# Four reorderings in a two-layer decoder kernel: copies ahead of a weight split, gate columns ahead of sums, sums behind a low part, and the last block in three pieces

## The chip, the cores and the metric

The kernel runs on one core of one Trainium2 chip. The metric is device microseconds (us) of one execution. A core has five engines with a queue each: TensorE (PE in the profile) multiplies matrices, VectorE (DVE), ScalarE (ACT) and GpSimd (POOL) work elementwise, and SyncE (SP) issues transfers. Each engine takes its instructions strictly in the order in which they were recorded, and waits on semaphores for the others.

## The reference

A trunk of two decoder layers over a residual stream `h` of 512 tokens by 1024 features, in float32. Each sublayer is normed before and after ("sandwich").

```python
for l in range(DEPTH):                       # DEPTH = 2
    g = norm_gains[l]
    if l < N_A:                              # layer 0: 12 heads in three groups (window, dilation)
        mix = dilated_mixer(rms_norm(h, g[0]), w_qkv_a[l], w_o_a[l], cos, sin)
    else:                                    # layer 1: 16 heads, keys and values from kvf
        if l == N_A:
            kvf = rms_norm(h, kv_norm) @ w_kvf
            ...
            log_f = jax.nn.log_sigmoid((kvf[..., 2 * B_WIDTH:] + b_f).astype(jnp.float32))
            c_sh = jnp.cumsum(log_f, axis=1) # gates: a bias c_q - c_k on the scores
        mix = fox_mixer(rms_norm(h, g[0]), w_q_b[j], w_o_b[j], k_sh, v_sh, c_sh)
    h = h + rms_norm(mix, g[1])
    f = conv_ffn(rms_norm(h, g[2]), w_up[l], conv_w[l], conv_b[l], w_down[l])
    h = h + rms_norm(f, g[3])
```

`conv_ffn` is an up projection to 5632 features, a causal convolution of width 3, a GELU gate, and a down projection from 2816 features.

## The kernel before

**Products in three passes.** A float32 product is made of three matmuls on operands that are split into a high part in fp32r and a low part, `mm3`: high by high, high by low, low by high (lines 276, 277, 278). So most of TensorE's rows come in threes. A weight piece of 128x1024 is loaded by SP (line 48) into a raw buffer; ACT casts it into the high part (line 56) and DVE subtracts that from the raw piece to get the low part (line 64). The class `Weights` does this ahead of need: `get()` hands out the next piece and first splits on until `ahead - 1` further pieces are ready; `split(n)` splits until `n` pieces are.

**Order by hand.** No scheduler moves anything: the order in which the Python code records instructions is the order on each engine. PSUM has eight banks of 128x512 float32; a new bank tile waits until the readers of the one before it in that bank are done.

**Place 1, layer 0's last projection.** `wide_proj(1, "v_ps", ...)` makes the values of two head groups in four banks and four steps `s`, each with one weight piece and 24 matmuls of 128x512. After each step stands a list of small work for the attention ("between"). In step 1 it is: transposes of queries and keys for blocks 2 and 3 of group 2 (`qk_transpose`, line 1045, each with a DVE copy out of PSUM, line 1048); scores of blocks 0 and 1 (`scores`, line 1072: two banks per block, then DVE's fused mask and minimum at line 1055 and ACT's exponential at line 1056); the transposes of block 3's probabilities of group 1 (`p_transpose`, line 1092, copied out by ACT at line 1094). The four banks that the values leave free serve all of these in turn. At the end of each step `next(down0)` does one stage of `down_sums`: sums and differences of quarters of the down-projection weights for a seven-product (Strassen-like) scheme, four DVE operations of 128x512 (lines 606 to 609), with loads by SP and stores to DRAM (`dT`, line 614).

**Place 2, the gates.** Before the second attention, the cumulative gates of 16 heads (tile `c8`) are transposed by TensorE (line 1620) and copied by DVE to `cq` (line 1622), a column for each head. POOL's `f_bias` (lines 1635, 1636) makes the bias of a score block from `cq` and `ck`. Here `down_sums` for layer 1 (`down1`) has its stores issued by POOL.

**Place 3, the end of the second attention.** The loop over 18 steps `m` ends with `f_out_low(7)` (line 1715), the low part of the last two heads' outputs, which is also the last reader of the bank `o_ps`. Then come the transposes of the convolution's columns (line 586) with their DVE copy (line 588), and the output projection `po.finish`, whose first `get()` splits eight pieces: four of `w_o_b`, four of `w_up`. The last of four sets of `down1` sums stood at `m = 17`, ahead of `f_out_low(7)`.

**Place 4, the last rows.** In the down projection of the last layer, the blocks of 128 tokens are finished in the order 2, 3, 0, 1. For a block, `p_11` makes the last nine matmuls of its first 512 columns and `p_12` those of the other 512. `Final` then squares and sums (ACT, line 316), multiplies by the gain (DVE, line 323: tile `mix`), and when the row's sum is known takes the root (ACT, 318), the reciprocal (DVE, 328), adds to `h` in two halves (DVE, 330) and stores each half (SP). For the last block, `narrow` cuts `p_12` into two parts of 256 columns, both in one bank.

Of the kernel before, what the change touches and what calls it, by code (L numbers as in the profile page):

```python
# [100 lines left out]
def trunk_kernel(ctx, tc, x, norm_gains, w_qkv_a, w_o_a, w_q_b, w_o_b, kv_norm, w_kvf, b_f,  # L101
# [199 lines left out]
    class Mix:  # L301
# [5 lines left out]
        def half(self, b, n, hf, o):  # L307
            if n == 0:
                self.st[b] = (small(2, "ss"), t4([128, D], name="mix"), small(1, "sd"), small(1, "vr"))
            self.part(b, n, o, H2[hf], n == 1)  # L310

        def part(self, b, n, o, s, last):

            ss, m, sd, v = self.st[b]
            junk = t2([128, 512], BF16, name="junk")
# [220 lines left out]
    class Final:  # L536
# [11 lines left out]
        def half(self, i, n, hf, o):  # L548
            self.mix.half(self.order[i], n, hf, o)
            if n:  # L550
                self.out(self.order[i])

        def part(self, b, n, o, s):
            self.mix.part(b, n, o, slice(512 + s.start, 512 + s.stop), n == 2)
            if n == 2:
                self.out(b)

# [73 lines left out]
    def ffn(l, bd, cp, nxt, ahead):  # L631
# [208 lines left out]
        def down(nxt, ahead):  # L840
# [39 lines left out]
            for i, b in enumerate(nxt.order):  # L880
                if ahead and i < 2:
                    W.split(W.n_split + 1)
                if b >= 2:
                    nxt.half(i, 0, 1, db[b, 1])
                    for j in range(ND - 2, ND):
                        p_21(j, b - 2)
                    nxt.half(i, 1, 0, db[b, 0])
                    for bp in range(2):
                        p_1(last[0] - 2 + i, bp)
                    if ahead and i == 1:  # L890
                        W.split(W.n_split + 1)
                    continue
                for j in last:
                    p_11(j, b)
                nxt.half(i, 0, 0, db[b, 0])
                parts = (slice(0, 256), slice(256, 512)) if nxt.narrow and i == NB - 1 else (slice(0, 512),)
                for q, part in enumerate(parts):
                    for j in last:
                        p_12(j, b, part)
                        if (i, j) == (NB - 1, last[1]) and getattr(nxt, "early", None):  # L900
                            nxt.early()
                    if len(parts) > 1:
                        nxt.part(b, 1 + q, db[b, 1][:, part], part)
                    else:
                        nxt.half(i, 1, 1, db[b, 1])

# [337 lines left out]

    def wide_proj(g, name, post, between):

        banks = [bank([128, T], name=name) for _ in range(4)]
        for s in range(4):
            w = W.get()
            wh, wl = (t.rearrange("p (k c) -> p k c", k=2) for t in w)  # L1250
            for b in range(4):
# [10 lines left out]
    def v_post(g, b, o):  # L1262
# [20 lines left out]
        [L(qk_transpose, 2, 0), L(qk_transpose, 2, 1), L(p_transpose, 1, 2)],  # L1283
        [L(qk_transpose, 2, 2), L(qk_transpose, 2, 3), L(scores, 2, 0), L(scores, 2, 1), L(p_transpose, 1, 3)],
        [L(scores, 2, 2), L(scores, 2, 3), L(p_transpose, 2, 0)],
        [factors, L(p_transpose, 2, 1), L(p_transpose, 2, 2), L(p_transpose, 2, 3)]])
    for g in range(2):
# [308 lines left out]
    for c in range(4, 8):  # L1596
# [17 lines left out]
        if c < 6:  # L1614
            next(gate)
        if c >= 6:
            next(down1)
# [3 lines left out]
    cq = sml.tile([128, 4, 16], F32, tag="cq", name="cq", bufs=1)  # L1621
    dve.tensor_copy(cq, cqp)
    load_ck(0)

# [105 lines left out]
    for m in range(M + 2):  # L1730
# [38 lines left out]
        if live and i0 == 2 and j:  # L1769
            f_out_low(j - 1)  # L1770
        if m >= M - 3:
            next(down1)

    f_out_low(7)
    W.ahead, W.ahead_dma = 4, 2
    cp = conv_columns(load_conv(1))
    bd = Boundary(load_gain(norm_gains[1, 1], "gain11"), load_gain(norm_gains[1, 2], "gain12"), "xc")
    po.finish(bd, 4)
# [45 lines left out]
```

## Time and profile before

| | |
|---|---|
| median of 3 runs | 1118.95 us (1118.54 to 1121.36) |
| the profiled execution | 1118.97 us, of which the span from first to last instruction is 1117.2 us |
| PE busy | 1104.7 us (99%), 6395 matmuls |
| DVE, ACT, POOL busy | 893.9 us (80%), 616.4 us (55%), 191.2 us (17%) |
| granted TensorE clock, mean | 0.996 |
| PE's waits in all | 6.2 us, in eight places |

Times in the profile's rows are us from the span's start. A timeline row gives start, duration, engine, line, operation, what it writes and reads, and in brackets the idle time before it and what ended that. Matmuls overlap: a row of 128x512 is shown with 0.39 us, and the next starts 0.23 us later. So work is counted here from start to start. A matmul on float32 operands (transposes, layer 0's scores) counts twice in the trace's numbers.

### The profile page before, as it was taken

How to read it: one execution, taken by the hardware profiler on the slowest of the kernel's cores; microseconds unless marked ns; L12 is line 12 of the kernel's file. 1: busy time of each engine (PE TensorE's matmuls, PEld its weight loads, DVE VectorE, ACT ScalarE, POOL GpSimd, SP SyncE). 2: the span in 40 equal slices, each digit the busy share in tenths (PEclk: the TensorE clock that was granted, in tenths of full speed). 3: DMA queues.
4: the chain of work that ended last, by engine and by line, in shares of the span. 5: the costliest groups of instructions: out<-in, count | busy, mean ns of one | idle time of the engine just before them, and what ended most of it. 6: DMA issues, size and time to landing. Idle time of an engine off the chain costs nothing.

```text
span 1117.2 us, 17530 instructions
## 1 busy us (share of the span) xinstructions
PE 1104.7 (99%) x6395; PEld 942.9 (84%) x6395; DVE 893.9 (80%) x1462; ACT 616.4 (55%) x1038; POOL 191.2 (17%) x287
## 2 busy tenths in 40 slices
PE   9999999999999999999999999999999999999997
PEld 6988789989989988888888788788889889888886
DVE  6577778888788589897877866968888888689994
ACT  5444466444454456576655677746545445456572
POOL 1832010400000121000010555411200000121000
PEclk9999999999999999999999999999999999999999
DMA  9469864334344499975762644894333443599862
GB/s 324 148 216 407 325 173 116 113 95 124 114 140 124 130 352 372 336 282 133 208 151 76 192 131 124 272 307 132 95 110 108 137 124 117 158 347 376 310 245 75
DMA packets 180464, 218.40 MB, mean 195 GB/s; under 512 B 11225, under 2 KB 131017, under 8 KB 180378
## 3 DMA queue, kind: packets, MB, share of 16 engines
q1 hardware_dynamic: 168698, 180.81, 49.1%
q0 software_dynamic: 11680, 36.48, 11.3%
q8 instruction: 50, 0.82, 0.3%
q14 instruction: 36, 0.29, 0.1%
HBM read 170.28 MB, written 39.63 MB: 188 GB/s over the span
## 4 chain that ended last, share of the span: by engine, by line
PE 92%; DVE 3%; ACT 2%; issue 1%; DMA 1%; SPq 0%; POOL 0%; DVEq 0%; ACTq 0%; POOLq 0%
PE up L276 13%; PE up L277 13%; PE up L278 13%; PE acc L276 7%; PE acc L278 7%; PE acc L277 7%; PE v_ps L276 2%; PE v_ps L277 2%; PE v_ps L278 2%; PE qk_ps L277 2%; PE qk_ps L276 2%; PE qk_ps L278 2%; PE first L278 1%; PE first L277 1%; PE first L276 1%; PE o_ps L1701 1%
## 5 line engine op out<-in xcount | busy, mean ns | idle before, releaser
L640 ACT ACTIVATE bb<-up,conv 128x512 f32<-128x512 f32 x80 | 60.6, 775 | 149.1 <-DVE up L967 76.2
L64 DVE TENSOR_TENSOR w<-wraw,w 128x1024 fp32r<-128x1024 f32 x94 | 121.1, 1314 | 26.5 <-ACT w L56 25.2
L56 ACT CAST w<-wraw 128x1024 fp32r<-128x1024 f32 x108 | 110.3, 1049 | 20.8 <-DMA wraw<-in_w_up_dram 8.1
L276 PE MATMUL acc<-w 128*128 128x512 f32 (+1 forms) x311 | 120.7, 388 | 1.1 <-DVE mix L323 1.1
L278 PE MATMUL acc<-w 128*128 128x512 f32 (+1 forms) x311 | 120.5, 387 | 0.0
L276 PE MATMUL up<-xch,w 128*128 128x512 f32 (+1 forms) x292 | 104.9, 359 | 0.0
L276 PE MATMUL up<-xbh,w 128*128 128x512 f32 (+1 forms) x292 | 104.9, 359 | 0.0
L277 PE MATMUL up<-xbl,w 128*128 128x512 f32 (+1 forms) x292 | 104.9, 359 | 0.0
L277 PE MATMUL up<-xcl,w 128*128 128x512 f32 (+1 forms) x292 | 104.9, 359 | 0.0
L278 PE MATMUL up<-xch,w 128*128 128x512 f32 (+1 forms) x292 | 104.7, 359 | 0.0
L278 PE MATMUL up<-xbh,w 128*128 128x512 f32 (+1 forms) x292 | 104.7, 359 | 0.0
L277 PE MATMUL acc<-w 128*128 128x512 f32 (+1 forms) x267 | 103.3, 387 | 0.0
L656 POOL DMA_DIRECT2D hD<-hc x42 | 24.2, 576 | 317.7 <-DVE hc L658 316.6
L276 PEld LDWEIGHTS acc<-w 128*128 128x128 f32 x311 | 58.4, 188 | 13.0 <-DVE mix L323 1.3
L278 PEld LDWEIGHTS acc<-w 128*128 128x128 f32 x311 | 58.4, 188 | 12.4 <-DVE w L768 0.4
L641 DVE SCALAR_TENSOR_TENSOR bb<-up,conv,bb 128x511 f32<-128x511 f32 x80 | 59.4, 743 | 7.8 <-ACT bb L640 7.8
L276 PE MATMUL up<-xsh,w 128*128 128x256 f32 x224 | 63.4, 283 | 0.0
L277 PE MATMUL up<-xsl,w 128*128 128x256 f32 x224 | 63.4, 283 | 0.0
L278 PE MATMUL up<-xsh,w 128*128 128x256 f32 x224 | 63.4, 283 | 0.0
L276 PEld LDWEIGHTS up<-xbh,w 128*128 128x128 f32 x292 | 55.1, 189 | 8.3
L643 DVE SCALAR_TENSOR_TENSOR bb<-up,conv,bb 128x510 f32<-128x510 f32 x80 | 59.9, 749 | 2.8
L276 PEld LDWEIGHTS up<-xch,w 128*128 128x128 f32 x292 | 55.1, 189 | 8.2
(325 smaller groups left out, 3032.8 us busy)
## 6 DMA issues: line engine op xcount, KB each, us to landing
wraw<-in_w_up_dram SPq DMA_DIRECT2D x88, 512.0 KB, 4.2
dT<-dsums SPq DMA_DIRECT2D x24, 512.0 KB, 6.5
dsums<-in_w_down_dram SPq DMA_DIRECT2D x22, 512.0 KB, 6.0
dsums<-in_w_down_dram SPq DMA_DIRECT2D x44, 256.0 KB, 7.2
hD<-hc POOLq DMA_DIRECT2D x44, 256.0 KB, 4.6
dact<-hD SPq DMA_DIRECT2D x44, 256.0 KB, 5.9
wraw<-dT SPq DMA_DIRECT2D x22, 512.0 KB, 7.3
wraw<-in_w_down_dram SPq DMA_DIRECT2D x22, 512.0 KB, 5.8
```

What stands on the lines that cost most here:

```text
L56: self.nc.scalar.copy(pair[:, 0], raw)
L64: self.nc.vector.tensor_tensor(pair[:, 1], raw, pair[:, 0].bitcast(F32), ALU.subtract)
L276: pe.matmul(o, ah, bh, start=first, stop=False, skip_group_check=shared)
L277: pe.matmul(o, ah, bl, start=False, stop=False, skip_group_check=shared)
L278: pe.matmul(o, al, bh, start=False, stop=last, skip_group_check=shared)
L640: act.activation(bb[:, s, :], ps, AF.Identity, bias=cp[:, 3, ch:ch + 1], scale=cp[:, 2, ch:ch + 1])
L641: dve.scalar_tensor_tensor(bb[:, s, 1:], ps[:, :T - 1], cp[:, 1, ch:ch + 1], bb[:, s, 1:], ALU.mult, ALU.add)
L643: dve.scalar_tensor_tensor(bb[:, s, 2:], ps[:, :T - 2], cp[:, 0, ch:ch + 1], bb[:, s, 2:], ALU.mult, ALU.add)
L656: pool.dma_start(hD[c - 1], hc.pop(c - 1))
L1701: pe.matmul(o[64 * hh:64 * hh + 64, i * 128:(i + 1) * 128], Vt[hd // 8][:, k, (hd % 8) * 64:(hd % 8) * 64 + 64], pT[j, i, hh][:, k, :], st ...
```

## The change

Four edits, each of order; no arithmetic is added or left out but one tiny add.

1. In step 1 of the value projection, `get()` splits one piece less (`ahead` 3 instead of 4). The piece is split later in the same step by `W.split(W.n_get + 3)`, which now stands behind the copies of the transposed queries and keys and behind `p_transpose(1, 3)`; that one is moved ahead of the scores.
2. The last `down1` stage before the second attention stands behind the transposes and the copy to `cq`, not ahead of them.
3. The last of the four `down1` stages in the attention's loop stands behind `f_out_low(7)` and the copy of the convolution's columns.
4. The last block's columns are made and treated as 512 to 768, then 0 to 512, then 768 to 1024, so that another bank's products lie between the two parts of one bank. The add and the stores of the block before are recorded behind the first of these pieces.

```diff
@@ class Mix
         def half(self, b, n, hf, o):
+            self.part(b, n, o, H2[hf], n == 1)
+
+        def part(self, b, n, o, s, last):
+
             if n == 0:
                 self.st[b] = (small(2, "ss"), t4([128, D], name="mix"), small(1, "sd"), small(1, "vr"))
-            self.part(b, n, o, H2[hf], n == 1)
-
-        def part(self, b, n, o, s, last):
...
@@ class Final
             self.mix.half(self.order[i], n, hf, o)
-            if n:
+            if n and i != 2:
                 self.out(self.order[i])
 
         def part(self, b, n, o, s):
-            self.mix.part(b, n, o, slice(512 + s.start, 512 + s.stop), n == 2)
-            if n == 2:
-                self.out(b)
+            self.mix.part(b, n, o, s, n == 2)
+            if n != 1:
+                self.out(b if n else self.order[2])
@@ def down
+                if nxt.narrow and i == NB - 1:
+                    for n, (start, stop) in enumerate(((512, 768), (0, 512), (768, 1024))):
+                        for j in last:
+                            if start:
+                                p_12(j, b, slice(start - 512, stop - 512))
+                            else:
+                                p_11(j, b)
+                        o = db[b, 1][:, start - 512:stop - 512] if start else db[b, 0]
+                        nxt.part(b, n, o, slice(start, stop))
+                    continue
...
@@ wide_proj
+            W.ahead = 3 if s == late else 4
             w = W.get()
+            W.ahead = 4
...
-        [L(qk_transpose, 2, 2), L(qk_transpose, 2, 3), L(scores, 2, 0), L(scores, 2, 1), L(p_transpose, 1, 3)],
+        [L(qk_transpose, 2, 2), L(qk_transpose, 2, 3), L(p_transpose, 1, 3), lambda: W.split(W.n_get + 3),
+         L(scores, 2, 0), L(scores, 2, 1)],
...
-        [factors, L(p_transpose, 2, 1), L(p_transpose, 2, 2), L(p_transpose, 2, 3)]])
+        [factors, L(p_transpose, 2, 1), L(p_transpose, 2, 2), L(p_transpose, 2, 3)]], 1)
@@ before the second attention
-        if c >= 6:
+        if c == 6:
             next(down1)
     cqp = bank([128, 4, 16], name="cq_ps")
...
     dve.tensor_copy(cq, cqp)
+    next(down1)
     load_ck(0)
@@ the attention's loop
-        if m >= M - 3:
+        if M - 3 <= m <= M:
             next(down1)
 
     f_out_low(7)
     W.ahead, W.ahead_dma = 4, 2
     cp = conv_columns(load_conv(1))
+    next(down1)
```

At place 1, DVE's queue around the copies of the transposed queries and keys (`qkT`), before. `dsums` are the weight sums, `w<-wraw,w` is the low part of a weight piece, and the row with the mask is the first operation on the scores:

```order
L607 TENSOR_TENSOR dsums<-dsums 128x512
L608 TENSOR_TENSOR dsums<-dsums 128x512
L609 TENSOR_TENSOR dsums<-dsums 128x512
L64 TENSOR_TENSOR w<-wraw,w 128x1024
L1048 COPY qkT_1200<-qkT_ps 128x512 x2
L1055 ISA p,st<-s_ps,mask_132 128x128
```

And with the change:

```order
L607 TENSOR_TENSOR dsums<-dsums 128x512
L608 TENSOR_TENSOR dsums<-dsums 128x512
L609 TENSOR_TENSOR dsums<-dsums 128x512
L1053 COPY qkT_1200<-qkT_ps 128x512 x2
L64 TENSOR_TENSOR w<-wraw,w 128x1024
L1060 ISA p,st<-s_ps,mask_132 128x128
```

The low part now stands between the copies and the scores' first operation. On ACT, the copy of `p_transpose(1, 3)` moves ahead of this piece's cast and of the exponentials of the scores; on PE, its transposes move ahead of the scores.

At place 2, DVE's queue at the end of the key projection, before (`cq` is the gates' columns, `kst` the last keys):

```order
L1376 TENSOR_TENSOR kst_5792<-k_ps,kst_5792 128x512
L606 TENSOR_TENSOR dsums<-dsums 128x512
L607 TENSOR_TENSOR dsums<-dsums 128x512
L608 TENSOR_TENSOR dsums<-dsums 128x512
L609 TENSOR_TENSOR dsums<-dsums 128x512
L1622 COPY cq<-cq_ps 128x64
L64 TENSOR_TENSOR w<-wraw,w 128x1024
```

And with the change:

```order
L1384 TENSOR_TENSOR kst_5792<-k_ps,kst_5792 128x512
L1630 COPY cq<-cq_ps 128x64
L606 TENSOR_TENSOR dsums<-dsums 128x512
L607 TENSOR_TENSOR dsums<-dsums 128x512
L608 TENSOR_TENSOR dsums<-dsums 128x512
L609 TENSOR_TENSOR dsums<-dsums 128x512
L64 TENSOR_TENSOR w<-wraw,w 128x1024
```

The copy is now ahead of the four sums. POOL's queue is the same in both: the two stores of these sums, then the first `f_bias`.

At place 4, the end of DVE's queue, before (`mix` is the row by its gain, `vr` the running sum of squares, `h` the output rows):

```order
L320 TENSOR_SCALAR vr<-ss 128x1
L323 TENSOR_TENSOR mix<-acc,gain_7819 128x512 x2
L328 RECIPROCAL rs<-sd 128x1
L330 TENSOR_SCALAR h<-mix,rs,h 128x512 x2
L320 TENSOR_SCALAR vr<-ss 128x1
L323 TENSOR_TENSOR mix<-acc,gain_7819 128x512
L322 TENSOR_TENSOR vr<-vr,ss 128x1
L323 TENSOR_TENSOR mix<-acc,gain_7819 128x256 x2
L328 RECIPROCAL rs<-sd 128x1
L330 TENSOR_SCALAR h<-mix,rs,h 128x512 x2
```

And with the change:

```order
L320 TENSOR_SCALAR vr<-ss 128x1
L323 TENSOR_TENSOR mix<-acc,gain_7819 128x512 x2
L320 TENSOR_SCALAR vr<-ss 128x1
L323 TENSOR_TENSOR mix<-acc,gain_7819 128x256
L328 RECIPROCAL rs<-sd 128x1
L330 TENSOR_SCALAR h<-mix,rs,h 128x512 x2
L322 TENSOR_TENSOR vr<-vr,ss 128x1
L323 TENSOR_TENSOR mix<-acc,gain_7819 128x512
L323 TENSOR_TENSOR mix<-acc,gain_7819 128x256
L328 RECIPROCAL rs<-sd 128x1
L330 TENSOR_SCALAR h<-mix,rs,h 128x512 x2
```

The block before the last has its reciprocal and its two adds between the first and the second piece of the last block. On PE, the nine matmuls of 128x256 of the first piece now stand ahead of the nine of 128x512, and the other nine of 128x256 behind them.

More of the change, by code (lines that the diff above doesn't have):

```diff
@@ L895, in down @@
                 nxt.half(i, 0, 0, db[b, 0])
[L896 to L905, printed above, removed]
+                for j in last:
+                    p_12(j, b)
+                    if (i, j) == (NB - 1, last[1]) and getattr(nxt, "early", None):
+                        nxt.early()
+                nxt.half(i, 1, 1, db[b, 1])
         def half_mm(o, w, x, s, start):
@@ L1243, in trunk_kernel, with wide_proj @@
     reorder(2, 3)
-    def wide_proj(g, name, post, between):
+    def wide_proj(g, name, post, between, late=None):
         banks = [bank([128, T], name=name) for _ in range(4)]
         for s in range(4):
+            W.ahead = 3 if s == late else 4
             w = W.get()
+            W.ahead = 4
             wh, wl = (t.rearrange("p (k c) -> p k c", k=2) for t in w)
```

## The prediction

> **What bounds the kernel now.** I read the page first, then PE's waits.
>
> ```profile
> PE 1104.7 (99%) x6395; PEld 942.9 (84%) x6395; DVE 893.9 (80%) x1462; ACT 616.4 (55%) x1038; POOL 191.2 (17%) x287
> PE s_ps L1072 <- DVE qkT L1048: 1.2, 1, 1.2
> PE acc L276 <- DVE mix L323: 1.1, 1, 1.1
> PE qk_ps L277 <- DVE w L64: 1.0, 2, 0.8
> PE o_ps L1701 <- ACT pT L1688: 0.7, 1, 0.7
> PE xt_ps L344 <- DVE xn L295: 0.4, 1, 0.4
> PE acc L276 <- DVE OTb L1715: 0.4, 1, 0.4
> ```
>
> The first row is TensorE's share of the span of 1117.2 us: 99%. The others give whom PE waited for: us in total, times, the longest. So no change of order can win more than PE's idle time, 6.2 us with the wait at the start, and what those waits cost beyond their own length. Four of these rows are the places of the four edits: `qkT` (place 1), `pT` (place 2), `OTb` (place 3), `mix` (place 4). Next I read place 1 on PE's timeline, and the granted clock in the windows around it.
>
> ```profile
> 119.19 0.72 PE L1072 MATMUL s_ps<-qkT 64*128 64x128 f32 x8
> 121.15 1.68 PE L1072 MATMUL s_ps<-qkT 64*128 64x128 f32 x8 [1.24 <-DVE qkT L1048]
> 130.01 1.26 PE L1072 MATMUL s_ps<-qkT 64*128 64x128 f32 x16
> 131.32 0.66 PE L1092 MATMUL pT_ps<-ident,p 128*128 128x128 f32 x4
> 137.29 1.47 PE L1092 MATMUL pT_ps<-ident,p 128*128 128x128 f32 x12
> ...
> 122.00:123.00 1.00, 1.00 (x5) 0.78 (x5) 1.00 (x11) 1.00 (x5) 0.00 (x0) 0.50 0.91 240
> 120.00:130.00 10.00, 8.85 (x36) 7.12 (x36) 7.29 (x24) 4.61 (x18) 0.00 (x0) 0.83 1.02 381
> 630.00:640.00 10.00, 9.22 (x63) 7.20 (x62) 9.81 (x32) 8.55 (x24) 8.58 (x16) 1.00 0.57 147
> ```
>
> In the window rows the number behind the five engines is the granted clock. PE stands still for 1.24 us ahead of the scores of block 1, since the third bank they need still holds transposes that DVE has not copied. Right behind that the clock is 0.50. Over 120 to 130 it is 0.83, which makes (1 - 0.83) x 10 / 0.5 = 3.4 us at half speed, a loss of 1.7 us. The wait of 0.74 us at 635 left the clock at 1.00.
>
> What the place costs in all: from 130.01 to 137.29 PE does the same work as from 119.19 to 130.01 (16 score passes, 4 transposes, 24 products), in 7.28 us. From 119.19 it took 10.82. So the stall with its slow clock costs 3.54 us, not 1.24.
>
> **Place 1: the copies first.** What PE waits for is DVE, which waits for ACT:
>
> ```profile
> 119.27 1.23 DVE L64 TENSOR_TENSOR w<-wraw,w 128x1024 fp32r<-128x1024 f32 x1 [2.72 <-ACT w L56]
> 120.41 1.28 DVE L1048 COPY qkT<-qkT_ps 128x512 f32<-128x512 f32 x2
> 121.61 0.28 DVE L1055 CUSTOM_DVE_ANT_0 p<-s_ps,mask 128x128 f32<-128x128 f32 x1
> 123.30 0.69 DVE L606 TENSOR_TENSOR dsums<-dsums 128x512 f32<-128x512 f32 x1
> 126.63 1.23 DVE L64 TENSOR_TENSOR w<-wraw,w 128x1024 fp32r<-128x1024 f32 x1 [0.46 <-ACT w L56]
> 130.75 0.29 DVE L1055 CUSTOM_DVE_ANT_0 p<-s_ps,mask 128x128 f32<-128x128 f32 x1 [2.90 <-PE s_ps L1072]
> ...
> 121.99 0.40 ACT L1056 ACTIVATE p<-p,st 128x128 f32<-128x128 f32 x1 [2.75 <-DVE st L1055]
> 125.09 0.56 ACT L1094 COPY PT<-pT_ps 128x512 f32<-128x512 f32 x1
> 125.55 1.05 ACT L56 CAST w<-wraw 128x1024 fp32r<-128x1024 f32 x1
> ```
>
> DVE had been idle for 2.72 us when it began the low part at 119.27, and only then came the copies. With the change they start when the transposes are there, the last by 119.2 (PE's next row starts at 119.19), and at 0.6 each (120.41 to 121.61 for both) they end by about 120.1, while PE does four transposes (0.42 from 131.32 to its next products) and the first scores. Bank by bank: the second score bank needs the first copy (about 119.5), the third the second copy (120.1), the fourth ACT's copy of `p_transpose(1, 3)`, done about 120.3. PE asks for them at about 119.9, 120.2 and 120.5, so the old wait is gone, and PE reaches the scores of step 2 at 119.19 + 7.28 = 126.47 instead of 130.01.
>
> What is late next is DVE, because the low part now stands between the copies and the scores' mask. I follow it with the durations above. The four transposes start at 119.19, their row is 0.66 long: ACT copies from 119.85, 0.46 later (125.09 to 125.55) it casts, from 120.31. The low part starts 1.08 after its cast (125.55 to 126.63): 121.39. The mask starts 1.14 behind it (119.27 to 120.41): 122.53, that is 0.92 later than before. The sums follow 1.69 behind (121.61 to 123.30), at 124.22, and take 2.87 (123.30 to 126.63 less the 0.46 of idling): 127.09. On ACT the exponentials start 0.38 behind the mask (121.61 to 121.99), at 122.91, and take 3.10; the next cast is at 126.01 and the next low part at 127.09. So the mask of step 2's scores can start at 127.09 + 1.14 = 128.23, where PE would have its scores ready from 126.47 on.
>
> Step 2's transposes need the bank of the first of these scores, and ran 0.57 behind the mask (130.75 to 131.32): 128.80. Undisturbed PE would be there 1.31 after the scores' start (130.01 to 131.32), at 127.78. So a **new wait of 1.02 us** takes the place of the old one, and PE is there at 128.80 instead of 131.32: **a gain of 2.52 us**. DVE and ACT are ahead by the same, and what follows follows them. The ends: 3.54 without a new wait, 0.8 if the new wait brings the half-speed stretch along (1.7 more). I take 2.52: the wait at 635, 0.74, left the clock alone, and 1.02 is not far above it.
>
> [...]
>
> **Place 2: gate columns first.**
>
> ```profile
> 623.54 0.69 DVE L609 TENSOR_TENSOR dsums<-dsums 128x512 f32<-128x512 f32 x1
> 624.15 0.22 DVE L1622 COPY cq<-cq_ps 128x64 f32<-128x64 f32 x1
> 624.29 1.21 DVE L64 TENSOR_TENSOR w<-wraw,w 128x1024 fp32r<-128x1024 f32 x1
> ...
> 624.53 0.53 POOL L614 DMA_DIRECT2D dT<-dsums  x1 [0.92 <-DVE cq L1622]
> 625.10 0.99 POOL L1635 TENSOR_SCALAR bias<-ck,cq 128x128 f32<-128x128 f32 x2
> ```
>
> `cq` is moved ahead of the sums on DVE, but POOL, which needs it, has the two stores of these very sums ahead of its first `f_bias`. The second store starts 0.30 behind the last sum's end (624.23), and the bias at once behind the store. So the bias never waited for `cq`, it waited for the sums. These now start 0.14 later (624.15 to 624.29, the copy). POOL, then DVE, then ACT pass this on to `pT`, and the wait at 635 grows from 0.74 to 0.88: **a loss of 0.14 us**. The ends: 0 and 0.3 (the copy's full 0.22 and a semaphore). A gain is excluded as long as POOL's order stands.
>
> **Place 3: the low part first.**
>
> ```profile
> 731.08 0.58 ACT L1711 CAST OTb<-o_ps 128x512 fp32r<-128x512 f32 x1 [2.39 <-PE o_ps L1701]
> 732.67 0.68 DVE L1715 TENSOR_TENSOR OTb<-o_ps,OTb 128x512 fp32r<-128x512 f32 x1
> 730.00:740.00 10.00, 9.58 (x59) 7.60 (x56) 8.12 (x10) 4.59 (x5) 1.59 (x3) 1.00 1.04 391
> 739.82 9.28 DMA wraw<-in_w_up_dram
> 756.48 0.76 DVE xn L295
> ```
>
> The second row is `f_out_low(7)`, for whose bank PE waits 0.42. It needs ACT's cast in the first row, which ends at 731.66; with one set of four sums less ahead of it, it can start by then, 1.01 earlier, and the wait goes. But the rows from the chain that ended last run elsewhere: from the load of a `w_up` piece (landing at 749.10) over its cast and low part to the normed rows `xn` at 756.48, for which PE waits 0.4 again (`xt_ps`). DMA is full at that time (share 1.04 from 730 to 740), and the bytes are the same. So PE comes 0.42 earlier to a point that does not come earlier: the wait there becomes 0.84, **a gain of 0**. The ends: 0.42 gained if DMA lands that much earlier, 1.86 lost if the moved sums (2.87 of DVE, less the 1.01) hold up the eight low parts behind them, thereby the raw buffers, and thereby the loads. I take 0, since DMA with a share above 1 is the nearer bound on that load.
>
> **Place 4: three pieces.**
>
> ```profile
> 1107.59 0.28 PE L276 MATMUL acc<-w 128*128 128x256 f32 x1
> 1108.54 0.28 PE L278 MATMUL acc<-w 128*128 128x256 f32 x1
> 1109.91 0.39 PE L276 MATMUL acc<-w 128*128 128x256 f32 x1 [1.09 <-DVE mix L323]
> 1110.97 0.28 PE L278 MATMUL acc<-w 128*128 128x256 f32 x1
> ...
> 1107.26 1.42 DVE L330 SCALAR_TENSOR_TENSOR h<-mix,rs,h 128x512 f32<-128x512 f32 x2
> 1111.84 0.42 DVE L323 TENSOR_TENSOR mix<-acc,gain 128x256 f32<-128x256 f32 x1 [1.98 <-ACT junk L316]
> ```
>
> These are the first and the last matmul of each part of 256 columns, then the add of the block before, and `mix` of the last part. The first part takes 0.95 from its first to its last start, 0.12 per matmul, so the second could have started at 1108.66. It started at 1109.91, 1.25 later, and took 1.06 from first to last: 1.36 us lost in all, since both parts lie in one bank that `mix` still read. In the new order nine matmuls of 512 (9 x 0.23 = 2.0 us) lie between, and `mix` of a part ends 1.3 after the part's last matmul started (1110.97 to 1112.26). Cover 2.1 against need 1.3: the wait goes, and the rows behind the last matmul are the same. The postponed add of the block before fits into those 2 us on DVE (1.42 us, which now runs ahead of the second piece's `mix`). **A gain of 1.36 us**; the ends are 1.0, if DVE's queue holds the last `mix` by 0.3, and 1.5.
>
> **The sum.** The profiled execution took 1118.97 us, as good as the median of 1118.95. 1118.97 - 2.52 + 0.14 - 0 - 1.36 = 1115.23: **1115.2 us**, 0.33% less. A measurement of this kernel can tell about 0.3% from no change, that is 3.36 us, with the line at 1115.6. The forecast lies just beyond it.
>
> **The rivals.**
> - **A, as summed** (chance 0.49): 1115.2, own range 1114.6 to 1116.0 from the small ends at places 2 to 4.
> - **B, no new wait at place 1** (0.12): DVE or ACT are quicker than the rows chained above. 1115.2 - 1.0 = 1114.2. Against it: each link is a row of the same stage.
> - **C, the slow stretch stays** (0.20): the new wait drops the clock as the old one did, or the timed runs of before did not all have the drop. 1.7 us less is won: 1116.9. For it: 1.02 us is not far from 1.24 either. Against the second form: two of the three times of before, 1118.54 and 1118.95, lie at the profiled one or 0.4 below, less than a drop. [...]
> - **D, place 3 holds up the loads** (0.08): 1115.2 + 1.86 = 1117.1. It decides from the point at which the raw buffers, not DMA, set the loads. For it: eight low parts are queued behind the moved sums. Against it: the share of 1.04.
> - **E, slower than before: the clock gives way at three waits** (0.05). Three waits are left or made: 1.02 at place 1, 0.88 at 635, 0.84 at 757. If from 0.8 us of idling on the clock drops for 3.4 us, each costs 1.7: 1115.2 + 5.1 = 1120.3, 0.12% above the median. It decides from the length of idling that drops the clock. Against it: 0.74 at 635 and the 0.8 in the row of `qk_ps` are nearly there, and I saw the drop behind the 1.24 alone.
> - **The change does not do what it says**: so it is at place 2, and that is in the sum. At places 1, 3 and 4 the queues do carry the new order.
>
> The rest (0.06) is unnamed, 0.04 of it slower. Faster by over 0.3%: 0.35 of A, all of B, 0.02 unnamed: 0.49. Within 0.3%: 0.14 of A, C, D, E: 0.47. Slower: 0.04. The range takes in A to D with 0.3 on both sides: 1113.9 to 1117.3.
>
> **What would show it.** Place 1: no wait for `qkT`; the clock at 1.00 between 118 and 126; a wait of about 1 us of the transposes `pT_ps` (line 1097) for DVE near 127.8; the `qkT` copies ending by 120.2. If that wait is under 0.4, the chain on DVE is wrong; if the clock falls behind it, C holds. Place 2: the first bias starts 0.1 to 0.2 later against the keys' last product, and the wait for `pT` is 0.8 to 1.0. Place 3: no wait for `OTb`, one of about 0.8 for `xn`. Place 4: no wait for `mix`, and the span's end 1.3 sooner behind the start of the last block. A total under 1113.9 would mean that a wait I count as renewed has gone for good; one over 1117.3, that a wait I do not see was made.

## The result, and the profile after

The change runs in **1115.89 us** (median of 7 runs, 1114.56 to 1118.54), the kernel before, beside it, in 1120.55 us (7 runs, 1118.54 to 1121.36). The ratio is 0.9969, with a 95% interval of 0.9958 to 0.9981: 0.3% faster, 0.7 us above the forecast of 1115.2 and inside its range. Between these medians the gain is 4.7 us, and 3.3 in the second series of the change below; the forecast, reckoned from the profiled 1118.97, was 3.7. Two runs of several ms, one of the kernel before and one of an experiment, are left out of all counts. The first profiled execution was the slowest of the seven, 1118.54 us, and that turned out to be instructive. PE's row and its waits in it (total, times, longest):

```profile
PE 1103.4 (99%) x6395; PEld 942.6 (84%) x6395; DVE 894.4 (80%) x1462; ACT 617.0 (55%) x1038; POOL 191.1 (17%) x287
PE xt_ps L344 <- DVE xn L295: 2.1, 1, 2.1
PE acc L278 <- DVE w L768: 1.1, 1, 1.1
PE pT_ps L1097 <- DVE st L1060: 0.8, 1, 0.8
PE o_ps L1710 <- ACT pT L1697: 0.7, 1, 0.7
```

The waits for `qkT`, `OTb` and `mix` are gone. `pT_ps` (line 1097) is the new wait forecast at place 1. `xt_ps` is 2.1 instead of the forecast 0.84, and the wait for a low part at line 768 is in no step of the prediction. Place 1 on the timeline, DVE first and then PE; next the clock (the number behind the engines) at place 1 and behind the wait for `xn`:

```profile
118.81 1.29 DVE L1053 COPY qkT<-qkT_ps 128x512 f32<-128x512 f32 x2 [2.30 <-PE qkT_ps L1050]
121.25 1.23 DVE L64 TENSOR_TENSOR w<-wraw,w 128x1024 fp32r<-128x1024 f32 x1 [1.15 <-ACT w L56]
122.39 0.28 DVE L1060 CUSTOM_DVE_ANT_0 p<-s_ps,mask 128x128 f32<-128x128 f32 x1
126.95 1.23 DVE L64 TENSOR_TENSOR w<-wraw,w 128x1024 fp32r<-128x1024 f32 x1
128.09 0.28 DVE L1060 CUSTOM_DVE_ANT_0 p<-s_ps,mask 128x128 f32<-128x128 f32 x1
...
119.58 1.45 PE L1077 MATMUL s_ps<-qkT 64*128 64x128 f32 x16
126.63 1.26 PE L1077 MATMUL s_ps<-qkT 64*128 64x128 f32 x16
128.74 0.63 PE L1097 MATMUL pT_ps<-ident,p 128*128 128x128 f32 x4 [0.85 <-DVE st L1060]
...
120.00:130.00 10.00, 9.15 (x62) 7.45 (x59) 8.74 (x40) 6.87 (x27) 0.00 (x0) 1.00 1.02 396
750.00:760.00 10.00, 7.85 (x31) 6.02 (x30) 8.51 (x17) 7.50 (x17) 0.00 (x0) 0.83 0.06 22
```

At place 1 the copies end at 120.10, the low part, the mask and the second low part follow as forecast, and PE waits 0.85 without losing the clock. Near 756 the clock is at half speed (0.50 in each us from 757 to 759) for (1 - 0.83) x 10 / 0.5 = 3.4 us, behind the 2.1 us of idling. The tail of the span, in order of time: the last matmul of the first piece, the first and last of the middle one, the first of the last piece, then `mix` of the last pieces:

```profile
1107.41 0.28 PE L278 MATMUL acc<-w 128*128 128x256 f32 x1
1107.53 0.40 PE L276 MATMUL acc<-w 128*128 128x512 f32 x1
1109.37 0.39 PE L278 MATMUL acc<-w 128*128 128x512 f32 x1
1109.60 0.28 PE L276 MATMUL acc<-w 128*128 128x256 f32 x1
...
1110.59 1.25 DVE L323 TENSOR_TENSOR mix<-acc,gain 128x512 f32<-128x512 f32 x2
```

No piece waits for the one before it. Every trace holds the same 6395 matmuls, so matmul k of one can be set against matmul k of another. Only inside places 1 and 4 does the change alter their order: matmul 632 is one of the scores in the kernel before and one of the transposes moved ahead of them in the change, but the gains come out the same, within 0.01, if they are reckoned from matmul 628, ahead of both. (In these counts only the scores' matmuls at place 1 stand twice. A transpose stands once: four for one `p_transpose`.) This table is worked out from the starts of single matmuls: where each execution stands against the profiled one of before, in us (a negative number is earlier). Several of its rows are experiments, told below.

```
ahead of / behind      place 1     place 2   place 3 at OTb  at xn  xn +12  l.768: before, behind  last block: first, last  
matmul no.            632    689   3500 3540   4200   4360    4452    4520     5900     5940          6360     6394
start in before    119.41 131.32 629.22 635.85 714.27 735.84 757.28  769.44   999.18  1008.51       1103.73  1110.97
change, 1st profile  -0.04  -2.58  -2.50 -2.50  -2.50  -3.50   -1.78   -0.16   -0.19     0.91          0.91    -0.42
change, 2nd profile  -0.33  -2.88  -2.47 -2.48  -2.47  -3.47   -3.06   -3.05   -3.08    -1.98         -1.97    -3.30
place 1 alone         0.71  -1.83  -1.75 -1.75  -1.75  -2.03   -2.17   -2.17   -2.18    -1.21         -1.20    -1.20
place 3 alone         0.19  -1.37  -1.29 -1.26  -1.27  -1.99   -2.08   -2.09   -2.12    -1.20         -1.21    -1.21
place 4 alone         0.11   0.13   0.21  0.23   0.24   0.22    0.17    0.17    0.15     1.72          1.72     0.39
change less place 3   0.14  -2.41  -2.34 -2.32  -2.32  -2.61   -2.96   -2.96   -2.98    -1.39         -1.40    -2.73
all mended            0.11  -3.14  -3.03 -3.86  -2.99  -3.96   -4.54   -4.82   -4.84    -5.10         -5.12    -6.45
```

The first column differs by what happens in the first 15 us of each execution (up to 0.7; the reason was not followed). A difference between two columns is what a stretch gives or costs.

### The profile page after: what moved, and what is told of

It is laid out like the page before. It is cut to its first block, busy times and chain, and to the rows that moved or that the text cites. A ratio compares the mean times of both kernels' runs of the same rounds, so it can differ in the third digit from the quotient of the medians.

```text
span 1116.7 us, 17530 instructions
## 1 busy us (share of the span) xinstructions
PE 1103.4 (99%) x6395; PEld 942.6 (84%) x6395; DVE 894.4 (80%) x1462; ACT 617.0 (55%) x1038; POOL 191.1 (17%) x287
## 4 chain that ended last, share of the span: by engine, by line
PE 90%; DMA 4%; ACT 2%; DVE 2%; issue 1%; SPq 1%; POOL 0%; DVEq 0%; ACTq 0%; POOLq 0%
PE up L276 12%; PE up L277 12%; PE up L278 12%; PE acc L276 8%; PE acc L278 8%; PE acc L277 8%; DMA dsums<-in_w_down_dram 2%; PE qk_ps L277 2%; PE qk_ps L276 2%; PE qk_ps L278 2%; PE v_ps L276 2%; PE v_ps L277 2%; PE v_ps L278 2%; PE o_ps L1710 2%; PE pT_ps L1695 2%; PE s_ps L1663 1%
```

## The experiments

**The edits one by one.** Place 1 alone, place 4 alone, place 3 alone, and the change without place 3: each takes the lines of the change's diff for its places and leaves the others as in the kernel before. Every experiment was timed beside its own runs of the kernel before, whose medians range from 1119.0 to 1120.4. So between two experiments, differences of about 1 us are read from the traces and not from the times; the intervals of the ratios of the change and of its single mends all overlap. Place 1:

```diff
-        [..., L(scores, 2, 0), L(scores, 2, 1), L(p_transpose, 1, 3)],
+        [..., L(p_transpose, 1, 3), lambda: W.split(W.n_get + 3), L(scores, 2, 0), L(scores, 2, 1)],
```

> The kernel before with the edit at place 1 alone. By the prediction: 2.5 us faster than before beside it, no wait for qkT, a wait of the transposes pT_ps of about 1 us near 127.8, no half-speed stretch behind it. By rival C (the slow clock moves to the new wait): 0.8 us faster, with a clock of about 0.83 in 126 to 136. By rival B (no new wait): 3.5 us faster.

1117.42 us (11 runs) against 1118.99 of before (31 runs), ratio 0.9983 (0.9974 to 0.9993). Local gain 0.71 + 1.83 = 2.54 us. The total gain of the medians is smaller, 1.6. Place 4:

```diff
-                parts = (slice(0, 256), slice(256, 512)) if nxt.narrow and i == NB - 1 else (slice(0, 512),)
+                    for n, (start, stop) in enumerate(((512, 768), (0, 512), (768, 1024))):
```

> The kernel before with the edit at place 4 alone. By the prediction: 1.36 us faster, no wait for mix. If the last mix is held up on the vector engine: 1.0. If the old wait brought a slow clock along that also goes (the window 1111 to 1112 of before had 0.89): up to 1.5.

1117.67 us (11 runs), ratio 0.9990 (0.9981 to 0.9999). In the table the last block gives 1.72 - 0.39 = 1.33. Place 3:

```diff
-        if m >= M - 3:
+        if M - 3 <= m <= M:
             next(down1)
     f_out_low(7)
     ...
+    next(down1)
```

> The kernel before with the edit at place 3 alone. By the prediction: 0, the wait of 0.4 for OTb goes and the one for xn grows from 0.4 to about 0.8. The rival from the trace of after: PE arrives 1 to 1.5 us earlier at xn, waits 1.5 to 2.1 there, and in those executions in which that drops the clock it loses 1.7 for 3.4 us at half speed, so 0 in some executions and 1.3 to 1.7 slower in others. By rival D (loads held up): 1.9 slower in every execution.

1120.04 us (12 runs), ratio 1.0003 (0.9995 to 1.0011): nothing, as forecast. (The median lies 1.0 above that of before since seven of the twelve runs are in the upper of two groups, of which more below.) But this trace brought something else. It has the old wait at place 1, since that edit is not in it, and yet no slow clock. First place 3 alone, then place 4 alone, the same wait in each, and the window behind it:

```profile
121.34 1.31 PE L1072 MATMUL s_ps<-qkT 64*128 64x128 f32 x8 [1.24 <-DVE qkT L1048]
120.00:130.00 10.00, 8.71 (x55) 6.97 (x53) 8.09 (x29) 4.84 (x19) 0.00 (x0) 1.00 1.02 390
```

```profile
121.26 1.50 PE L1077 MATMUL s_ps<-qkT 64*128 64x128 f32 x8 [1.24 <-DVE qkT L1053]
120.00:130.00 10.00, 8.76 (x38) 7.07 (x36) 7.39 (x24) 4.62 (x18) 0.00 (x0) 0.83 1.02 385
```

So the wait of 1.24 us sometimes slows the clock and sometimes does not. Without the drop this stretch takes 0.19 + 1.37 = 1.56 us less than in the profile of before. The times fall into two groups that agree. Of place 3 alone, five runs lie at 1117.6 to 1118.6 and seven at 1120.0 to 1121.1, and the profile without the drop (1117.73) is of the lower group. Of place 4 alone, six lie at 1115.9 to 1117.7 and five at 1118.9 to 1119.5, and the profile with the drop (1119.33) is of the upper one. With the edit at place 1 alone, which takes the wait away, ten of eleven runs lie together, at 1116.7 to 1118.0, and one at 1120.3.

Of the 69 repeats of before beside the experiments, 32 have a mean granted clock of 0.997 or less, and their median time is 1120.3; 37 have 0.998 or more, and theirs is 1118.6. So the drop is in about half of them. This is an estimate: the mean is over the whole span and also counts the end of it, where the clock falls behind the last matmul (0.89 from 1111 to 1112 in before), and place 4 alone, whose profile has the drop, has a mean of 0.998.

> The change without its edit at place 3. By the prediction: as the change, 3.7 faster than before. By the rival from the trace of after (the wait of 2.1 for xn with a slow clock behind it is place 3's doing): 1.7 faster than the profiled execution of the change (1118.54), near 1116 and always so, and no slow clock at 755 to 760. By rival D: 5.6 faster than before.

1115.62 us (7 runs), ratio 0.9973 (0.9962 to 0.9983), as the change itself.

**The change again, for a second profile.**

> The change itself once more, for its times beside the variants and a second profile. If the 2.1 us wait for xn with a slow clock behind it, in the first profile of the change, is an accident of that execution: a wait of 0.3 to 0.8 there, no slow clock, and times near 1115.8. If it is the change's: the same wait again and the times in two groups, near 1115.8 and 1118.5.

1115.79 us (7 runs, two of them at 1117.1 and 1118.3), ratio 0.9971 (0.9960 to 0.9982). Its wait for `xn`, and its window there:

```profile
PE xt_ps L344 <- DVE xn L295: 0.8, 1, 0.8
750.00:760.00 10.00, 9.16 (x44) 7.17 (x44) 8.79 (x17) 7.22 (x19) 0.00 (x0) 1.00 0.14 51
```

So the 2.1 us and the slow clock behind it are not in every execution of the change. Whether the two slower runs of this series had them, no profile shows.

**Is it the length of the wait that slows the clock?** The kernel before, with one copy of `qkT` made twice:

```diff
-        dve.tensor_copy(qkT[g][:, b], o)
+        for _ in range(2 if (g, b) == (2, 2) else 1):
+            dve.tensor_copy(qkT[g][:, b], o)
```

> The kernel before, with one of the two copies of qkT in step 1 of the value projection done twice, so that TensorE's wait for it grows by 0.6, from 1.24 to 1.84 us. Theory of chance: the wait of 1.24 slows the clock (3.4 us at half speed, 1.7 us lost) in about half the executions of before, and a longer wait does it more often: the times lose their lower group, and the median is 0.6 + 0.5 x 1.7 = 1.4 us above that of before, with most runs between 1120 and 1122. Rival: the two groups of before's times have another cause, and the clock has nothing to do with the wait's length: two groups again, both 0.6 higher, and the median 0.6 higher.

```profile
121.91 1.73 PE L1073 MATMUL s_ps<-qkT 64*128 64x128 f32 x8 [2.06 <-DVE qkT L1049]
120.00:130.00 10.00, 8.09 (x28) 6.75 (x29) 8.01 (x25) 4.60 (x18) 0.00 (x0) 0.66 1.03 399
```

1121.1 us against 1119.07, ratio 1.0014 (1.0005 to 1.0023). Of ten runs three lie at 1118.7 to 1119.2 and seven at 1120.7 to 1122.2. So the lower group did not vanish; it lies about 0.7 higher than that of the runs of before beside it, as the rival has it. That the drop comes more often after a longer wait (seven of ten here, nine of 21 of those runs of before by their mean clock) is not shown by so few runs. In the profiled execution the half speed lasted (1 - 0.66) x 10 / 0.5 = 6.8 us, twice the 3.4 of before.

**Place 1 without its new wait, first try.** `get()` splits one piece less in step 2 too, and the split stands behind everything else in that step:

```diff
-        [L(scores, 2, 2), L(scores, 2, 3), L(p_transpose, 2, 0)],
+        [L(scores, 2, 2), L(scores, 2, 3), L(p_transpose, 2, 0), lambda: W.split(W.n_get + 3)],
```

> The change, with the split of step 2 of the value projection also put behind that step's scores and transposes, so that on the vector engine no low part stands ahead of the mask of step 2. By the prediction's chain the mask then follows the sums at 126.95 instead of 128.09, the wait for it (0.85 in the trace of the change) goes or falls under 0.1, and the time is 0.8 us under the change's, about 1115.1. Rival: the cast and the low part are then late for step 3, whose weights PE waits for: no gain, and a wait for w at line 276 to 278 between 133 and 140. Rival B of the prediction (without the new wait the old stall is won whole): in executions of before with the slow clock 3.5, otherwise 1.8.

```profile
PE o_ps L1146 <- DVE V L1274: 0.8, 1, 0.8
PE f_ps L1162 <- DVE fac L1132: 0.3, 1, 0.3
...
132.50 1.22 DVE L64 TENSOR_TENSOR w<-wraw,w 128x1024 fp32r<-128x1024 f32 x1 [3.27 <-ACT w L56]
```

1116.20 us, ratio 0.9969 (0.9958 to 0.9981), no gain over the change. The wait for the mask went, and two others, of 0.8 and 0.3, came, since ScalarE's cast was moved too and DVE sat idle for 3.27 us for it. From matmul 632 to 3500 this execution gains 1.0 us less than the change's second profile.

**Second try: only the low part behind the masks**, with the cast where it was:

```diff
-        [L(scores, 2, 2), L(scores, 2, 3), L(p_transpose, 2, 0)],
+        [W.high, L(scores, 2, 2), L(scores, 2, 3), W.low, L(p_transpose, 2, 0)],
```

> The change, with the low part of step 2 of the value projection (vector engine) behind the masks of that step, its cast on ScalarE staying where it was. In the second split later, cast and low part both came late, and waits for V (0.8) and fac (0.3) took the place of the one for the mask. Here only the order on the vector engine changes. Expected: the mask follows the sums at about 127, the wait of 0.85 at line 1097 goes, none for V: 0.8 under the change, about 1115.0. Rival: the vector engine's work of the stage is the bound (busy 3.9 of 4 us from 124 to 132), and the wait only moves to V or to w again: about 1115.8, as the change.

```profile
128.79 0.63 PE L1097 MATMUL pT_ps<-ident,p 128*128 128x128 f32 x4
755.01 1.32 PE L344 MATMUL xt_ps<-ident,xn 128*128 128x128 f32 x8 [1.47 <-DVE xn L295]
750.00:760.00 10.00, 8.52 (x41) 6.70 (x40) 8.47 (x17) 7.86 (x20) 0.00 (x0) 1.00 0.14 44
```

1115.68 us (5 runs), ratio 0.9965 (0.9952 to 0.9977). The wait is gone and none for `V` came: from matmul 632 to 689 it is 0.70 faster than the change. But this execution waits 1.47 for `xn`, and the 0.7 does not reach the end.

**Place 2 with GpSimd's stores out of the way:**

```diff
     dve.tensor_copy(cq, cqp)
-    next(down1)
...
     f_bias(0, 0)
     f_bias(0, 1)
+    next(down1)
```

> The change, with the last sums ahead of the second attention (and so their two stores on GpSimd) put behind the first two biases, not only behind the copy to cq. If place 2 won nothing because of the stores ahead of the bias on GpSimd: the first bias starts 3.6 us earlier (619.1 instead of 622.7), the wait of 0.74 for pT at line 1710 goes, and the time is 0.7 under the change's, about 1115.2. Rival: the bias was not what the softmax waited for (its scores are there only at 623.2, 0.9 before the mask), and the wait falls only by part, 0.2 to 0.4. Rival: the sums behind the bias hold up the masks on the vector engine, no gain.

The first two biases and the stores, on GpSimd, in the change and then here:

```profile
622.16 0.53 POOL L614 DMA_DIRECT2D dT<-dsums  x1 [0.92 <-DVE dsums L609]
622.74 0.86 POOL L1644 TENSOR_SCALAR bias<-ck,cq 128x128 f32<-128x128 f32 x2
```

```profile
619.82 2.54 POOL L1643 TENSOR_SCALAR bias<-ck,cq 128x128 f32<-128x128 f32 x2 [3.52 <-DMA ck<-cd]
625.10 1.12 POOL L614 DMA_DIRECT2D dT<-dsums  x2
636.41 0.50 PE L278 MATMUL q_ps<-xqh,w 128*128 128x512 f32 x1 [0.23 <-DMA w<-wraw]
```

1115.85 us (8 runs), ratio 0.9969 (0.9958 to 0.9979), as the change. The first bias now waits for the load of `ck`, but the wait of 0.74 for `pT` is gone, and PE is 0.85 further ahead there. Of this 0.5 comes back soon behind it, at a weight whose transfer GpSimd issues (the last row, from one start to the next), and behind `xn` it stands where the change's second profile does (-3.02 against -3.06).

**What sets xn.** Place 3 carried further: the last sums with their stores behind the output projection.

```diff
     cp = conv_columns(load_conv(1))
-    next(down1)
...
     po.finish(bd, 4)
+    next(down1)
```

> The change, with place 3 carried further: the last sums and their two stores of 512 KB stand behind the whole output projection, so that these stores do not share DMA with the w_up pieces. If DMA's bytes set xn (the prediction's reason for a gain of 0 at place 3): the fourth w_up piece lands up to 1 MB / 0.39 MB per us = 2.7 us earlier, the wait of 0.8 for xn goes, and the time is 0.8 under the change's, about 1115.0. Rival: the low parts on the vector engine or PE itself set xn: the wait stays at 0.8, the time at 1115.8. Rival: the sums, 2.87 us of the vector engine, now stand ahead of the next stage's work and make a wait there of up to 2: about 1117.

The transfers issued between 720 and 757 (times, KB each, us to landing), the last cast (ACT) and low part (DVE) of a `w_up` piece and the first `xn`, in the change's second profile and then here:

```profile
dT<-dsums POOLq DMA_DIRECT2D x6, 512.0 KB, 8.6
wraw<-in_w_up_dram SPq DMA_DIRECT2D x6, 512.0 KB, 8.5
...
746.11 1.05 ACT L56 CAST w<-wraw 128x1024 fp32r<-128x1024 f32 x1 [0.67 <-DMA wraw<-in_w_up_dram]
747.20 1.23 DVE L64 TENSOR_TENSOR w<-wraw,w 128x1024 fp32r<-128x1024 f32 x1 [0.50 <-ACT w L56]
753.42 1.41 DVE L295 SCALAR_TENSOR_TENSOR xn<-h,rs,gain 128x512 f32<-128x512 f32 x2
```

```profile
wraw<-in_w_up_dram SPq DMA_DIRECT2D x6, 512.0 KB, 7.6
dT<-dsums POOLq DMA_DIRECT2D x4, 512.0 KB, 8.6
...
744.13 1.05 ACT L56 CAST w<-wraw 128x1024 fp32r<-128x1024 f32 x1 [0.73 <-DMA wraw<-in_w_up_dram]
745.21 1.22 DVE L64 TENSOR_TENSOR w<-wraw,w 128x1024 fp32r<-128x1024 f32 x1 [0.56 <-ACT w L56]
751.58 1.41 DVE L295 SCALAR_TENSOR_TENSOR xn<-h,rs,gain 128x512 f32<-128x512 f32 x2
```

1114.71 us (5 runs), ratio 0.9960 (0.9946 to 0.9974). With two stores of 512 KB less in front, the last low part is 1.99 us earlier and `xn` 1.84, though PE stood 0.7 later at place 3 in this execution, and the wait for `xn` is gone. The edit also takes 2.87 us of sums from ahead of the low parts on DVE. That is not what held `xn`: in both profiles DVE stands idle ahead of this low part for ACT, and ACT for the load. So the loads set `xn`, and the bytes beside them set the loads (8.5 us to landing with six stores beside them, 7.6 with four).

**The wait at line 768.** On DVE the sums of one pair (lines 754 to 756), which wait for a load of `hD`, are queued ahead of low parts that wait for nothing. They are put behind:

```diff
         def pair_sums(j):
-            pair_load(j + 1)
+            if j + 1 not in acts:
+                pair_load(j + 1)
...
                             pair_highs(c - NF + 2)
-                            pair_sums(c - NF + 3)
+                            if c == NF - 1:
+                                pair_load(3)
+                            else:
+                                pair_sums(c - NF + 3)
...
         post(*before, lambda: pair_lows(1))
+        pair_sums(2)
         pair_highs(2)
```

> The change, with the sums of the third dact pair (lines 754 to 756) ahead of layer 1's and layer 0's down projection put behind the low parts of pair 1. In all profiles but the first of before TensorE waits 0.9 to 1.6 us for such a low part (line 768) near 1006; on the vector engine there stand ahead of it sums that idle 1.3 to 2.1 us for a load of hD. If that order is the cause: the wait goes, and the time is 1.0 under the change's, about 1114.8. Rival: the loads of hD or of the sums are late themselves, and TensorE waits for the next pair instead: no gain.

DVE in the change's second profile, then here (where that code has moved down a line):

```profile
999.58 0.43 DVE L755 TENSOR_TENSOR dact<-dact 128x256 f32<-128x256 f32 x1 [1.95 <-DMA dact<-hD]
1002.42 2.35 DVE L768 TENSOR_TENSOR w<-wraw,w 128x1024 fp32r<-128x1024 f32 x2
1004.69 1.22 DVE L768 TENSOR_TENSOR w<-dact,w 128x1024 fp32r<-128x1024 f32 x1
```

```profile
999.91 2.35 DVE L769 TENSOR_TENSOR w<-wraw,w 128x1024 fp32r<-128x1024 f32 x2
1002.17 1.22 DVE L769 TENSOR_TENSOR w<-dact,w 128x1024 fp32r<-128x1024 f32 x1
1005.10 0.41 DVE L755 TENSOR_TENSOR dact<-dact 128x256 f32<-128x256 f32 x1
```

1115.35 us (5 runs), ratio 0.9965 (0.9953 to 0.9978). The low parts are 2.5 us earlier, and the wait is gone: against before, matmuls 5900 to 5940 go from -1.99 to -2.26, where the change goes from -3.08 to -1.98, 1.4 us better. Between the medians of the two series there is 0.4, which the times cannot resolve. This profile waits 1.3 for `xn`, the second one of the change 0.8.

**All four mends together.**

> The change with four mends together: the last sums behind the output projection, the low part of step 2 behind its masks, the last sums ahead of the attention behind the first two biases, and the third dact pair's sums behind the low parts. Measured alone against the change's second profile: wait for xn gone (0.8), wait for the mask gone (0.7), wait for pT gone with 0.5 left after a later wait for a weight, wait at line 768 gone (1.1). If with the stores out of the way xn no longer swallows what is won ahead of it, these add up to 3.1: about 1112.7. Rival: DMA still sets xn, the 1.2 won ahead of it is swallowed there, and only 0.8 + 1.1 are won: about 1113.9.

```profile
PE 1101.5 (99%) x6395; PEld 941.7 (85%) x6395; DVE 894.2 (81%) x1462; ACT 617.4 (56%) x1038; POOL 193.9 (17%) x287
PE qk_ps L277 <- DVE w L64: 1.0, 2, 0.7
PE q_ps L278 <- DMA w<-wraw: 0.6, 1, 0.6
```

**1112.83 us** (5 runs, 1112.50 to 1113.36) against 1120.40, ratio 0.9933 (0.9919 to 0.9948): 3.0 us under the change, against an expected 3.1. Reckoned from the runs of before beside each, it is 2.9 to 4.3 us, and its interval no longer overlaps the change's. (Left out of the rows is the wait of 1.4 at the very start.)

The table tells where it comes from. Against the change's second profile, from matmul 632 to 6394, this execution wins 0.7 at place 1, 0.3 from there to 4200, 1.25 from 4200 to 4520 (around `xn`) and 1.4 at line 768. Three of the four mends come out whole, once the wait for `xn` no longer takes back what is won ahead of it. The mend at place 2 does not: 0.83 is won from 3500 to 3540, and 0.87 is lost again by 4200, most of it at the weight of the last row.

## Why the prediction was right, and where it was not

**Place 1: the chain was right, the value of the stall was one of two.** The mask of step 2 was put at 128.23 and came at 128.09, the transposes at 128.80 and 128.74, the new wait at 1.02 and 0.85. The gain against the profiled execution was put at 2.52; the table gives 2.54, 2.55, 2.54 and 2.55 in the four rows that have the edit as it stands in the change. The step that failed is the one under C, "two of the three times of before lie at the profiled one or 0.4 below, less than a drop", so that the drop was taken to be in all executions. By the mean clock it is in about 0.46 of them. Against an execution without it the gain is 2.54 - 1.56 = 0.98, on the average 0.98 + 0.46 x 1.56 = 1.7, and place 1 alone measured 1.6 between the medians. C's second form held by half.

**Why the total still fitted.** The profiled execution of before had the drop, but no wait of PE's matmuls at line 768. Of the twelve profiles in which that stage is as it was, it is the only one without; the others have 0.9 to 1.6, place 4 alone among them (1.6), which is the kernel before up to its last block. The two accidents nearly cancel: a typical execution has 0.54 x 1.56 = 0.8 less of the one and about 1.1 more of the other. So 1118.97 stood well for the kernel before, whose medians were 1119.0 to 1120.6, but by luck. On the side of the change luck helped too: its second profile loses 0.41 from place 1 to 4200 and 1.10 at line 768, gets 0.59 back from 4200 to 4452 and 0.33 in the first 15 us, none of them in the sum, and so ends 3.30 ahead of the profiled execution of before, where the sum has 3.74. The prediction did not ask which waits of one trace are typical; another profile of the same kernel would have told.

**Place 2: the direction was right, the loss was not seen.** Against PE the first bias came 0.14 later (622.74 against 625.10, while PE was 2.50 earlier), just the price set. The wait for `pT` stayed at 0.74, and matmuls 3500 to 3540 moved by 0.02 or less. The 0.14 was taken up by the bias operations themselves: the first two took 0.86 where they had taken 0.99, and the next operation of GpSimd started at 623.67 against 626.17, 2.50 earlier, as PE was. That GpSimd's stores were the obstacle for `pT` is shown by the mend; that removing it wins time is not.

**Place 3: nothing won, for the reason given.** The wait for `OTb` went, and PE got 1.00 ahead there, where the change without the edit gets 0.29: 0.7 won, more than the 0.42 of the wait alone. `xn` took it back. From matmul 4200 to 4452 the seven profiles with the edit (without the two that also move the stores) changed by -0.28 on the mean, from -0.81 to +0.72, and the five without it by -0.26, from -0.64 to 0.00. Without the first profile, which has the half speed there, the six with the edit come to -0.44; that the edit wins this 0.2, the times neither show nor exclude. The forecast wait of 0.84 is the 0.8 of the second profile. Its size varies from execution to execution, 0.3 to 2.1 in the profiles with the edit, by more than the edit moves it. D, the loads held up in every execution, is ruled out by place 3 alone; E's drop at `xn` is in one profile, the first, at 2.1 us and not at the 0.8 that E assumed.

**Place 4: right.** Put at 1.36, measured 1.33 in each profile with the edit (1.72 to 0.39, 0.91 to -0.42, -1.97 to -3.30, -1.40 to -2.73). The postponed add found its room on DVE.

**B, no new wait,** did not come by itself, but could be had: moving the low part alone gives another 0.7, which shows in the time only when `xn` does not set it.

## What to carry to other kernels

Ask of a wait not only what it costs, but whether it is in every execution: a second profile of the unchanged kernel, or the spread of its times, tells it. A meeting point that the loads set, here `xn`, swallows what is won ahead of it, so it is to be freed first, here by moving stores that went beside these loads. When the second half of a piece of work is put later on one engine, try leaving the first half on the other engine where it was: here the wait only moved when both were put later.

## What the chip showed beyond the expected

**The same wait drops the clock in one execution and not in another.** The same 1.24 us of idling at the same place gave 3.4 us at half speed in two profiles and none in a third. Waits of 0.8 to 0.9 at place 1 left the clock alone in the four profiles whose clock was read there (1.00 from 120 to 130 in both profiles of the change, in place 1 alone and in the change without place 3), one of 2.06 gave 6.8 us, one of 2.1 at `xn` 3.4 us, one of 1.47 there nothing (its window 750 to 760 above). Length alone does not decide: at line 768 waits of 1.6 us, in place 4 alone and in the change without place 3, left the clock at 1.00 as well. Here is that of the latter, and the clock behind it:

```profile
1006.55 0.50 PE L278 MATMUL acc<-w 128*128 128x512 f32 x1 [1.57 <-DVE w L768]
1008.00:1009.00 1.00, 1.00 (x6) 0.81 (x6) 0.93 (x3) 0.49 (x1) 0.00 (x0) 1.00 0.99 366
```

By the clock records in the traces of the kernel before and of the change (its first profile), the half speed behind a wait lasted 3.413 us in each, and every change of clock lies a whole number of steps of 3.4133 us (112.64 / 33) behind the first record. Before, that record is at 9.28, the half speed begins 33 steps later (121.92) and ends at the 34th, and the clock falls behind the last matmul at the 323rd; with the change it is 9.03 and the steps 219 (756.55), 220 and 324. Before, the wait of 1.24 begins 1.4 us into a step. In place 4 alone the clock, 0.72 from 120 to 125, puts the start of the half speed at about 122.2, and the wait 1.2 into a step, if the same grid holds there: an estimate. For the waits without a drop in place 3 alone and in the change without place 3, no change of clock near them gives their place in the steps, so whether that place counts was not shown. The wait at place 1 stands between matmuls of 64 rows, that at line 768 between full ones; whether this counts was not tried, and the cause stays open.

**The same GpSimd operations took three times as long in another place.** The two first bias operations took 0.86 us in the change and 2.54 in the run with the sums behind them, where they ran beside VectorE's low part and sums (619.8 to 622.4). They began 2.9 us earlier by the clock of the span, but the block of bias that they start ended only 0.9 earlier (623.16 against 624.08). The cause was not tried apart.
